# A one-core decoder layer: how its first transfers are queued and how its last norm is finished

## The chip, the cores and the metric

The kernel runs on one core of a Trainium2 chip. The metric is the device time of one launch in microseconds (us), taken as the median of several runs. A separate, profiled execution of the same program gives the trace that is read below.

## What is computed

One decoder layer on 512 tokens of width 1024, in float32. The input is multiplied by one wide matrix, whose columns are shared out among a gated spatial branch (A), a differential attention (B) and two merge gates. The result is projected, added to the scaled input and to a gated embedding, and normalized:

```
h = x @ w_in[i]
ua, va, za, qh, kh, vh, zb, ga, gb = jnp.split(h, IN_OFFSETS, axis=-1)
...
q = apply_rope(qh..., cos, sin) * (B_QK_DIM ** -0.5)      # cos, sin from positions
...
merged = jax.nn.sigmoid(ga) * (ya @ w_branch_a[i]) + jax.nn.sigmoid(gb) * (yb @ w_branch_b[i])
mix_out = merged @ w_out[i]
ple = jax.nn.sigmoid(x @ w_ple_gate[i]) * (p[i] @ w_ple[i])
x = layer_norm(DEEPNORM_ALPHA * x + mix_out + ple, ln_g[i], ln_b[i])
```

Two places matter here: the very first product (`x` times the columns of `k` and `q`), with the sine tables that are made from the positions beside it, and the `layer_norm` at the end.

## The kernel before

Every float32 operand of the large products is cut into a high and a low part (`cut`, lines 293 to 298: ScalarE copies the high part, VectorE subtracts to get the low one; for the first block of `x` VectorE does both). Each product is then three matmuls on TensorE. Weights come in units of 128 x 1024 floats from DRAM into `wr` buffers (line 360), and are cut into `wh` and `wl`.

**The start.** `x` arrives transposed, in eight blocks `xr[0]` to `xr[7]` of 128 x 512 (256 KB each, line 487), and the first product runs over these blocks in order: 12 matmuls for each block, which need that block and half of a weight unit. SyncE (the profile calls its queue SPq) issues the transfers in this order: `xr[0]`; `xr[1]`; the second half of unit 0; `xr[2]`; a half of unit 1; `xr[3]`; the other half of unit 1; `xr[4]`; and so on. ScalarE's queue issues the first half of unit 0, in two pieces, at the same time as SyncE issues `xr[0]`. `xr[1]` is held back by hand: GpSimd (POOL) writes one column of it with a memset (line 505), and the transfer that overwrites this column waits for that. Since SyncE issues in order, all its later transfers wait too. In GpSimd's queue the memset stands behind the making of `ident` and `mask` and two small constants. After the memset GpSimd issues five transfers of its own (lines 538 and 540): `invf` (128 frequencies) and `pos`, the 512 positions, each group of 128 of them repeated over 32 partitions. VectorE turns both into angles (lines 544 to 552) in the middle of its cuts, and from these come the tables of sines and cosines.

**In between.** The order of everything else is set by an agenda that counts matmuls: `later(n, fn)` runs `fn` after `n` more matmuls have been issued. It is not touched.

**The end.** The last product (`out`) gives four rows of 128 tokens, t = 0 to 3. For each, VectorE adds the product to `base` (line 1374), takes statistics (line 1375), and calls `last_norm`: aggregate them to mean and variance `mv` (line 1176); add epsilon to the variance, on GpSimd here (`ve`, line 1178); raise it to the power -0.5 on GpSimd (`rs`, line 1180); meanwhile VectorE subtracts the mean and multiplies by `lg` (line 1381), and then multiplies by `rs` and adds `lb` (line 1385); SyncE stores (line 1386). The last row's statistics come in three pieces (512, 256 and 256 columns), and it is stored in three: 512, 256 and 256 columns. The same `rstd_of` serves the norm in branch A, with VectorE adding the epsilon.

Of the kernel before, what the change touches and what calls it, by code (L numbers as in the profile page):

```python
# [18 lines left out]
OP = mybir.AluOpType  # L19
# [217 lines left out]
def hybrid_layer(ctx: ExitStack, tc: tile.TileContext, a, out: bass.AP):  # L237
# [248 lines left out]
    def ask_xr(k):  # L486
        sp.dma_start(out=xr[:, k, :], in_=a["xT"][k * P:(k + 1) * P, :])
# [2 lines left out]

    ident = consts.tile([P, P], F32, name="ident")
    make_identity(nc, ident)
    attn, turning = ExitStack(), ExitStack()
    ap_ = attn.enter_context(tc.tile_pool(name="attn", bufs=1))
    rp = turning.enter_context(tc.tile_pool(name="turning", bufs=1, side="right"))
# [5 lines left out]
    pool.memset(mhalf, -0.5)  # L501
    halfpi = consts.tile([P, 1], F32, name="halfpi")
    pool.memset(halfpi, math.pi / 2)

    pool.memset(xr[:, 1, 0:1], 0.0)
    for k in range(1, KT):
        ask_xr(k)
        if k < 6:
            next(arrive[k // 2])

    cs = rp.tile([P, T], F32, name="cs")
    sn = rp.tile([P, T], F32, name="sn")
# [14 lines left out]
    def rope_tables():  # L527

        pos = rp.tile([P, P], I32, name="pos", tag="m", bufs=6)
        ang = rp.tile([P, P], F32, name="ang", tag="m", bufs=6)  # L530
        n = rp.tile([P, P], F32, name="nn", tag="m", bufs=6)
        made = [rp.tile([P, P], F32, name="made", tag="m", bufs=6) for _ in range(2)]
        spread_out = dram.tile([2, P, P], F32, name="tables")
        magic = 1.5 * 2.0 ** 23
        near = float(np.float32(2 * math.pi))

        def ask_positions():
            pool.dma_start(out=invf, in_=a["invf"])
            for c in range(NT):
                pool.dma_start(out=pos[c * HALF:(c + 1) * HALF, :],  # L540
                             in_=bcast(a["pos"][:, c * P:(c + 1) * P], P, HALF))

        def angles():
            dve.tensor_copy(ang, pos)
            dve.tensor_scalar(out=ang, in0=ang, scalar1=invf[:, 0:1], scalar2=None, op0=OP.mult)

        def reduce(parts):
            dve.tensor_scalar(out=n, in0=ang, scalar1=1.0 / (2 * math.pi), scalar2=magic,
                              op0=OP.mult, op1=OP.add)
            dve.tensor_scalar(out=n, in0=n, scalar1=magic, scalar2=None, op0=OP.subtract)  # L550
            for c in parts:
                dve.scalar_tensor_tensor(out=ang, in0=n, scalar=-c, in1=ang, op0=OP.mult, op1=OP.add)

        def sines():
            pi32 = float(np.float32(math.pi))
            dve.tensor_scalar(out=ang, in0=ang, scalar1=pi32, scalar2=-pi32, op0=OP.min, op1=OP.max)
            dve.scalar_tensor_tensor(out=n, in0=ang, scalar=-1.0, in1=ang, op0=OP.mult, op1=OP.max)
            act.activation(made[0], ang, AF.Sin)
            act.activation(made[1], n, AF.Sin, bias=halfpi[:, 0:1], scale=-1.0)

        def put():
            for i, t in enumerate(made):
                act.dma_start(out=spread_out[i], in_=t)

        def get():
            for i, (queue, t) in enumerate(((sp, sn), (pool, cs))):
                for u in range(4):
                    queue.dma_start(out=t[u:P:4, :].rearrange("f (c j) -> f c j", c=NT),
                                   in_=spread_out[i].rearrange("(c f) j -> f c j", c=NT))

        ask_positions()
        yield
        angles()
        reduce(two_pi_parts())
        yield
        reduce((near, float(np.float32(2 * math.pi - near))))
        for after, fn in zip(TABLES, (sines, put, get)):
            later(after, fn)
        yield

    tables = rope_tables()
    next(tables)
    cuts = [prep(u, halves) for u in range(3)]
    cuts[0] = prep(0, (0, P, T, 2 * T))
    for k in range(KT):
# [585 lines left out]
    later(AUX[3], load_bs)  # L1171
    later(AUX[4], mask_ws)

    def rstd_of(st, eps_by=dve):
        mv = small([P, 2], "mv")
        dve.bn_aggr(out=mv, in_=st)  # L1176
        ve = small([P, 1], "ve")
        eps_by.tensor_scalar(out=ve, in0=mv[:, 1:2], scalar1=EPS, scalar2=None, op0=OP.add)  # L1178
        rs = small([P, 1], "rs")
        pool.tensor_tensor(out=rs, in0=ve, in1=mhalf[:, 0:1], op=OP.pow)  # L1180
        return mv, rs

    def va_done(c, t, z, source):
# [190 lines left out]
        dve.tensor_tensor(out=z, in0=bank, in1=z, op=OP.add)  # L1374
        dve.bn_stats(out=zst[t][:, piece if n == T else piece - 1, :], in_=z)

    def last_norm(t, cuts, stores):
        mv, rs = rstd_of(zst[t], pool)
        for c in cuts:
            z = base[:, t, c]  # L1380
            dve.scalar_tensor_tensor(out=z, in0=z, scalar=mv[:, 0:1], in1=lg[:, c],
                                     op0=OP.subtract, op1=OP.mult)
        for c in stores:
            z = base[:, t, c]
            dve.scalar_tensor_tensor(out=z, in0=z, scalar=rs[:, 0:1], in1=lb[:, c], op0=OP.mult, op1=OP.add)  # L1385
            sp.dma_start(out=out[t * P:(t + 1) * P, c], in_=z)
# [8 lines left out]
    for t in range(NT):  # L1395
        ts = slice(t * P, (t + 1) * P)
        n = T if t < NT - 1 else T // 2
        for j in range(T // n):
# [5 lines left out]
                m = slice((k % 2) * T + j * n, (k % 2) * T + (j + 1) * n)  # L1404
                three(bank[:, :n], mh[:, k, ts], ml[:, k, ts], h[:, m], l[:, m], k == 0, k == KT - 1)
            later(1, residual, t, T // n + j, n, bank[:, :n])
        whole, parts = [slice(0, D)], [slice(0, T), slice(T, T + 2 * P), slice(T + 2 * P, D)]
        later(1, last_norm, t, whole, whole if t < NT - 1 else parts)
    flush()


# [39 lines left out]
```

## Time and profile before

| | us |
|---|---|
| median of 3 runs (624.39 to 626.04) | 624.63 |
| the profiled execution's own time | 622.83 |
| its span, from the first to the last instruction | 621.1 |
| TensorE busy in the span | 610.3 (98%) |

The profiled execution took 622.83 us, of which 1.73 lie outside the span. It lies 1.80 below the median of the runs. Times in the rows below count from the start of the span. A matmul's recorded length overlaps the next one's, so back-to-back matmuls are read by their starts. "Idle before" is time in which an engine did nothing, with the instruction whose end released it.

### The profile page before, as it was taken

How to read it: one execution, taken by the hardware profiler on the slowest of the kernel's cores; microseconds unless marked ns; L12 is line 12 of the kernel's file. 1: busy time of each engine (PE TensorE's matmuls, PEld its weight loads, DVE VectorE, ACT ScalarE, POOL GpSimd, SP SyncE). 2: the span in 40 equal slices, each digit the busy share in tenths (PEclk: the TensorE clock that was granted, in tenths of full speed). 3: DMA queues.
4: the chain of work that ended last, by engine and by line, in shares of the span. 5: the costliest groups of instructions: out<-in, count | busy, mean ns of one | idle time of the engine just before them, and what ended most of it. 6: DMA issues, size and time to landing. Idle time of an engine off the chain costs nothing.

```text
span 621.1 us, 8650 instructions
## 1 busy us (share of the span) xinstructions
PE 610.3 (98%) x3036; PEld 514.0 (83%) x3036; DVE 456.1 (73%) x780; ACT 326.5 (53%) x528; POOL 137.5 (22%) x145
## 2 busy tenths in 40 slices
PE   8999999999999999999999999999999999999994
PEld 5888888888888888888889988888888888888884
DVE  5897876878878866856678978577667759476486
ACT  5546564554654655478666765557467446132200
POOL 2173114534534521321012120111210000000022
PEclk9999999999999999999999999999999999999998
DMA  8579999697796699669799898999988976752002
GB/s 280 205 198 209 282 307 293 228 250 242 232 242 231 197 325 267 171 233 302 276 286 260 224 244 229 242 249 306 254 197 278 363 247 230 257 182 102 1 34 102
DMA packets 49915, 143.77 MB, mean 231 GB/s; under 512 B 6416, under 2 KB 7760, under 8 KB 49552
## 3 DMA queue, kind: packets, MB, share of 16 engines
q1 hardware_dynamic: 38640, 109.99, 50.1%
q0 software_dynamic: 8352, 28.64, 25.2%
q10 hardware_dynamic: 2880, 4.59, 2.0%
q8 instruction: 24, 0.39, 0.3%
q14 instruction: 19, 0.16, 0.1%
HBM read 120.00 MB, written 34.73 MB: 249 GB/s over the span
## 4 chain that ended last, share of the span: by engine, by line
PE 96%; DVE 1%; DMA 1%; POOL 1%; ACT 0%; issue 0%; POOLq 0%; DVEq 0%; ACTq 0%
PE ps_pp L271 55%; PE ps_sc L271 18%; PE ps_tx L271 9%; PE ps_sc L820 3%; PE ps_po L865 3%; PE ps_po L271 3%; PE ps_tr L271 3%; PE ps_tr L854 1%; DMA xr<-in_xT 1%; PE ps_tr L1207 1%; PE ps_po L1207 1%; PE ps_tx L904 0%; POOL ve L1178 0%; DVE base L1385 0%; PE ps_pp L1354 0%; PE ps_sc L1354 0%
## 5 line engine op out<-in xcount | busy, mean ns | idle before, releaser
L403 DVE TENSOR_TENSOR wl<-wr,wh 128x1024 fp32r<-128x1024 f32 (+1 forms) x136 | 167.6, 1236 | 61.0 <-ACT wh L400 58.9
L400 ACT ACTIVATE wh<-wr 128x1024 fp32r<-128x1024 f32 (+1 forms) x136 | 139.6, 1033 | 79.2 <-PE ps_po L271 19.4
L271 PE MATMUL ps_pp<-xh,wh 128*128 128x512 f32 (+1 forms) x276 | 109.4, 398 | 1.5 <-ACT wh L297 1.5
L271 PE MATMUL ps_pp<-xl,wh 128*128 128x512 f32 (+1 forms) x276 | 106.7, 388 | 0.0
L271 PE MATMUL ps_pp<-xh,wl 128*128 128x512 f32 (+1 forms) x276 | 105.4, 383 | 0.0
L271 PEld LDWEIGHTS ps_pp<-xh,wh 128*128 128x128 f32 x276 | 52.3, 190 | 10.5 <-ACT wh L297 2.6
L833 ACT ACTIVATE p<-p,sth 128x128 f32<-128x128 f32 (+3 forms) x64 | 35.6, 557 | 46.5 <-DVE sth L831 46.5
L271 PEld LDWEIGHTS ps_pp<-xh,wl 128*128 128x128 f32 x276 | 52.1, 189 | 9.0 <-DVE wl L298 0.4
L271 PEld LDWEIGHTS ps_pp<-xl,wh 128*128 128x128 f32 x276 | 52.2, 189 | 7.4
L375 POOL DMA_DIRECT2D wr<-in_w x26 | 22.6, 870 | 106.1 <-DVE wl L403 81.3
L1178 POOL TENSOR_SCALAR ve<-mv 128x1 f32<-128x1 f32 x4 | 5.3, 1316 | 153.3 <-DVE mv L1176 153.3
L827 DVE CUSTOM_DVE_ANT_0 p<-ps_sc,mask 128x128 f32<-128x128 f32 (+3 forms) x64 | 31.0, 484 | 6.2 <-PE ps_sc L820 5.7
L271 PE MATMUL ps_pp<-wl,xh 128*128 128x512 f32 x84 | 32.9, 391 | 0.0
L271 PE MATMUL ps_pp<-wh,xl 128*128 128x512 f32 x84 | 32.8, 390 | 0.0
L271 PE MATMUL ps_pp<-wh,xh 128*128 128x512 f32 x84 | 32.7, 389 | 0.0
L271 PE MATMUL ps_sc<-wl,xsh 128*128 128x512 f32 x80 | 31.2, 390 | 0.0
L271 PE MATMUL ps_sc<-wh,xsl 128*128 128x512 f32 x80 | 31.1, 389 | 0.0
L271 PE MATMUL ps_sc<-wh,xsh 128*128 128x512 f32 x80 | 31.1, 389 | 0.0
L271 PE MATMUL ps_pp<-wh,xsh 128*128 128x512 f32 x64 | 24.9, 389 | 0.0
L271 PE MATMUL ps_pp<-wl,xsh 128*128 128x512 f32 x64 | 24.9, 389 | 0.0
L271 PE MATMUL ps_pp<-wh,xsl 128*128 128x512 f32 x64 | 24.9, 389 | 0.0
L865 PEld LDWEIGHTS ps_po<-v,at 128*128 128x128 f32 x160 | 22.8, 190 | 2.3
(367 smaller groups left out, 1418.6 us busy)
## 6 DMA issues: line engine op xcount, KB each, us to landing
wr<-in_w SPq DMA_DIRECT2D x83, 512.0 KB, 5.0
wr<-in_w POOLq DMA_DIRECT2D x22, 512.0 KB, 7.4
k<-hl SPq DMA_DIRECT2D x16, 256.0 KB, 2.6
q<-hl SPq DMA_DIRECT2D x16, 256.0 KB, 4.8
ws_va<-in_w POOLq DMA_DIRECT2D x8, 512.0 KB, 11.2
ws_wb<-in_w POOLq DMA_DIRECT2D x8, 512.0 KB, 8.3
wr<-ws_va SPq DMA_DIRECT2D x8, 512.0 KB, 8.2
wr<-ws_wb SPq DMA_DIRECT2D x8, 512.0 KB, 4.5
```

The lines of the kernel that those rows point to most:

```text
L271: pe.matmul(ps, s, m, start=start, stop=stop, skip_group_check=read_within)
L375: pool.dma_start(out=raw[u][:, :n], in_=weights(STEPS[FOLLOWS[u]][1], n), accum_op=OP.add)
L400: act.activation(h, raw[u][:, :width(STEPS[u][0])], AF.Copy)
L403: dve.tensor_tensor(out=l, in0=raw[u][:, :width(STEPS[u][0])], in1=h.bitcast(F32), op=OP.subtract)
L820: pe.matmul(sc[m][:, :n], q[:, m, i * P:(i + 1) * P], kk[:, m, :n], start=o == 0, stop=o == 1)
L827: dve.tensor_tensor_reduce(out=pr[m][:, :n], in0=sc[m][:, :n], in1=mask[:, T - n:], scale=-(DK ** -0.5), scalar=3e38, op0=OP.add, op1=OP.m ...
L833: act.activation(pr[m][:, :n], pr[m][:, :n], AF.Exp, bias=st[:, m:m + 1], scale=-1.0, accum_out=st[:, 2 + m:3 + m])
L854: pe.transpose(tr[:, j * P:(j + 1) * P], ad[:, j * P:(j + 1) * P], ident)
L865: pe.matmul(po[:, i * P:(i + 1) * P], at[:, j * P:(j + 1) * P], v[:, j, h * P:(h + 1) * P], start=j == 0, stop=j == i)
L1178: eps_by.tensor_scalar(out=ve, in0=mv[:, 1:2], scalar1=EPS, scalar2=None, op0=OP.add)
L1207: pe.matmul(sa[:, t * P:(t + 1) * P], va[:, t, g * P:(g + 1) * P], aux[0][:, 0, g, :], start=True, stop=True)
```

## The change

1. The memset that holds `xr[1]` back moves up in GpSimd's queue: it stands right behind the making of `ident`, ahead of `mask` and the constants.
2. The positions and frequencies are asked for by SyncE, in two transfers instead of five by GpSimd: `pos` in one, whose source lists 4 groups, each repeated 32 times, of 128 numbers; then `invf`. They stand behind the second half of unit 1, ahead of `xr[4]`.
3. VectorE adds the epsilon in the last norm too, into `mv` itself; the tile `ve` is gone (for branch A's norm as well, where VectorE did it already).
4. The last row is finished and stored in two pieces of 512 columns, and the subtraction of the mean (line 1381) is cut in two like that as well; before it was one instruction, followed by three pieces.

```
-    pool.memset(xr[:, 1, 0:1], 0.0)          (behind mask, mhalf, halfpi)
+    pool.memset(xr[:, 1, 0:1], 0.0)          (behind make_identity)
...
         def ask_positions():
-            pool.dma_start(out=invf, in_=a["invf"])
-            for c in range(NT):
-                pool.dma_start(out=pos[c * HALF:(c + 1) * HALF, :],
-                             in_=bcast(a["pos"][:, c * P:(c + 1) * P], P, HALF))
+            positions = a["pos"]
+            sp.dma_start(out=pos, in_=bass.AP(tensor=positions.tensor, offset=positions.offset,
+                                              ap=[[P, NT], [0, HALF], [1, P]]))
+            sp.dma_start(out=invf, in_=a["invf"])
...
     tables = rope_tables()
-    next(tables)
+    for k in range(1, KT):
+        ask_xr(k)
+        if k < 6:
+            next(arrive[k // 2])
+        if k == 3:
+            next(tables)
...
-    def rstd_of(st, eps_by=dve):
+    def rstd_of(st):
         mv = small([P, 2], "mv")
         dve.bn_aggr(out=mv, in_=st)
-        ve = small([P, 1], "ve")
-        eps_by.tensor_scalar(out=ve, in0=mv[:, 1:2], scalar1=EPS, scalar2=None, op0=OP.add)
+        dve.tensor_scalar(out=mv[:, 1:2], in0=mv[:, 1:2], scalar1=EPS, scalar2=None, op0=OP.add)
         rs = small([P, 1], "rs")
-        pool.tensor_tensor(out=rs, in0=ve, in1=mhalf[:, 0:1], op=OP.pow)
+        pool.tensor_tensor(out=rs, in0=mv[:, 1:2], in1=mhalf[:, 0:1], op=OP.pow)
...
-        whole, parts = [slice(0, D)], [slice(0, T), slice(T, T + 2 * P), slice(T + 2 * P, D)]
-        later(1, last_norm, t, whole, whole if t < NT - 1 else parts)
+        later(1, last_norm, t, [slice(0, D)] if t < NT - 1 else [slice(0, T), slice(T, D)])
```

SyncE's queue near its beginning, before, from `xr[2]` on (`wr_121` is unit 1, `wr_126` unit 2; a name in brackets is the semaphore that the transfer waits for: the transfers of SyncE and ScalarE take eight of them in turn, so each waits for the landing of the one eight places earlier):

```order
L487 DMA xr<-in_xT 128x512
L360 DMA wr_121<-in_w 128x512 [waits DMAHW0_49]
L487 DMA xr<-in_xT 128x512 [waits DMAHW1_49]
L360 DMA wr_126<-in_w 128x512 [waits DMAHW2_49]
L487 DMA xr<-in_xT 128x512 [waits DMAHW3_49]
L360 DMA wr_126<-in_w 128x512 [waits DMAHW4_49]
L487 DMA xr<-in_xT 128x512 [waits DMAHW5_49]
```

The same place in the changed kernel (`wr_127` is unit 1, `wr_140` unit 2):

```order
L487 DMA xr<-in_xT 128x512
L360 DMA wr_127<-in_w 128x512 [waits DMAHW0_49]
L535 DMA pos<-in_pos 128x1x128 [waits DMAHW1_49]
L537 DMA invf<-in_invf 128x1 [waits DMAHW2_49]
L487 DMA xr<-in_xT 128x512 [waits DMAHW3_49]
L360 DMA wr_140<-in_w 128x512 [waits DMAHW4_49]
L487 DMA xr<-in_xT 128x512 [waits DMAHW5_49]
```

The two small transfers have pushed `xr[4]` and all behind it by two places: `xr[4]` now waits for the semaphore of `xr[1]` (number 3), which `xr[5]` waited for before.

GpSimd's queue at its beginning, before:

```order
masks.py:199 AFFINE_SELECT ident<-ident 128x128 [waits Pool_49]
L497 MEMSET mask 128x512
L498 AFFINE_SELECT mask<-mask 128x128 [waits Pool_49]
L501 MEMSET mhalf 128x8
L503 MEMSET halfpi 128x1
L505 MEMSET xr 128x1
L538 DMA invf<-in_invf 128x1
L540 DMA pos<-in_pos 32x128 x4
```

And in the changed kernel:

```order
masks.py:199 AFFINE_SELECT ident<-ident 128x128 [waits Pool_49]
L494 MEMSET xr 128x1
L499 MEMSET mask 128x512
L500 AFFINE_SELECT mask<-mask 128x128 [waits Pool_49]
L503 MEMSET mhalf 128x8
L505 MEMSET halfpi 128x1
L564 DMA cs<-tables 32x4x128 [waits DMAHW0_49]
```

The memset of `xr` has moved ahead of four instructions, and the five transfers are gone.

VectorE's last instructions, before, from the last piece of the product on:

```order
L1374 TENSOR_TENSOR base<-ps_pp,base 128x256 [waits PE_49]
L1375 BN_STATS vst<-base 128x6 [waits DVE_49]
L1176 BN_AGGR mv<-vst 128x2 [waits DVE_49]
L1381 SCALAR_TENSOR_TENSOR base<-base,mv,lg 128x1024 [waits DVE_49]
L1385 SCALAR_TENSOR_TENSOR base<-base,rs,lb 128x512 [waits DVE_49,Pool_49]
```

And in the changed kernel:

```order
L1374 TENSOR_TENSOR base<-ps_pp,base 128x256 [waits PE_49]
L1375 BN_STATS vst<-base 128x6 [waits DVE_49]
L1177 BN_AGGR mv<-vst 128x2 [waits DVE_49]
L1178 TENSOR_SCALAR mv<-mv 128x1 [waits DVE_49]
L1381 SCALAR_TENSOR_TENSOR base<-base,mv,lg 128x512 x2
L1385 SCALAR_TENSOR_TENSOR base<-base,rs,lb 128x512 [waits DVE_49,Pool_49]
L1385 SCALAR_TENSOR_TENSOR base<-base,rs,lb 128x512 [waits DVE_49]
```

The epsilon has come in ahead of the subtraction of the mean, on the engine that does both; line 1385 still waits for GpSimd, where only the power is left.

## Rows read from the trace of the kernel before

**Rows 1.** Busy time of each engine in two stretches of the span: the stretch, its length, then for each engine the busy us and the number of instructions, the granted clock as a share of full speed, the DMA engines' share, and GB/s.

```profile
9.50:78.00 68.50, 68.50 (x301) 56.42 (x302) 58.56 (x81) 40.40 (x54) 22.23 (x20) 1.00 0.84 239
613.06:621.10 8.04, 0.00 (x0) 0.00 (x0) 3.95 (x8) 0.00 (x0) 1.88 (x2) 0.71 0.34 130
```

**Rows 2.** Everything that TensorE waited for in the whole span: us in total, times, longest.

```profile
PE ps_pp L271 <- ACT wh L297: 1.5, 1, 1.5
PE ps_po L475 <- DVE zeros L472: 1.2, 1, 1.2
```

**Rows 3.** The chain of work that ended last, at its beginning, in order of time: start, us, what.

```profile
1.36 0.49 POOL mask L497
...
2.30 0.04 POOL xr L505
...
2.36 5.72 DMA xr<-in_xT
...
8.17 0.63 ACT xh L297
...
8.82 0.64 ACT wh L297
...
9.50 2.61 PE ps_pp L271 x9
```

**Rows 4.** Transfers issued from 2.0 to 2.7 us (`xr[1]`), from 2.7 to 3.0 (the second half of unit 0), and in the first 10 us those of `pos`: size, and us from issue to landing (the median where there are several); below them GpSimd's timeline for the issue of `pos`: start, us.

```profile
xr<-in_xT SPq DMA_DIRECT2D x1, 256.0 KB, 5.7
...
wr<-in_w SPq DMA_DIRECT2D x1, 256.0 KB, 6.1
...
pos<-in_pos POOLq DMA_DIRECT2D x4, 16.0 KB, 6.5
...
3.04 2.29 POOL L540 DMA_DIRECT2D pos<-in_pos  x4
```

**Rows 5.** The last matmul of the first block of `x`, from TensorE's timeline: start, us.

```profile
7.59 0.39 PE L271 MATMUL ps_tx<-xh,wl 128*128 128x512 f32 x1
```

**Rows 6.** VectorE's cut of the weights for the block of `xr[4]`, and the first of its pairs of cuts for the third step of `v`; with, from the chain, TensorE's block of `xr[4]` and its first two steps of `v` on those banks (24 matmuls to a step); start, us.

```profile
13.94 0.69 DVE L298 TENSOR_TENSOR wl<-wr,wh 128x512 fp32r<-128x512 f32 x1
...
48.48 2.35 DVE L403 TENSOR_TENSOR wl<-wa,wh 128x1024 fp32r<-128x1024 f32 x2
...
18.24 2.04 PE ps_pp L271 x9
...
45.44 8.16 PE ps_pp L271 x36
```

**Rows 7.** The DMA engines in the first 10 us, in slices of 0.25 us: their busy share in tenths, and GB/s.

```profile
DMA  0000000934999965536938959579899999999999
GB/s 0 0 0 0 0 0 0 106 68 162 330 406 363 406 244 72 57 66 172 124 98 205 189 172 221 156 188 291 307 361 402 393 410 406 414 389 381 422 332 385
```

**Rows 8.** SyncE's queue: the issue of `xr[4]`, and that of `xr[5]`, eight transfers after `xr[1]`; start, us.

```profile
5.12 0.81 SPq L487 DMA_DIRECT2D xr<-in_xT  x1
...
8.10 0.33 SPq L487 DMA_DIRECT2D xr<-in_xT  x1
```

**Rows 9.** The chain of work that ended last, in its last part, in order of time: start, us, what.

```profile
614.02 0.25 DVE mv L1176
...
614.34 1.31 POOL ve L1178
...
616.34 0.75 DVE base L1385
```

**Rows 10.** The last row's instructions on VectorE (timeline), SyncE's last stores (timeline), and the transfers of line 1386 by size with us to landing.

```profile
614.29 1.29 DVE L1381 SCALAR_TENSOR_TENSOR base<-base,mv,lg 128x1024 f32<-128x1024 f32 x1
...
616.34 1.54 DVE L1385 SCALAR_TENSOR_TENSOR base<-base,rs,lb 128x512 f32<-128x512 f32 x3 [0.77 <-POOL rs L1180]
...
617.12 1.30 SPq L1386 DMA_DIRECT2D out<-base  x3
...
out<-base SPq DMA_DIRECT2D x3, 512.0 KB, 2.6
out<-base SPq DMA_DIRECT2D x1, 256.0 KB, 2.0
out<-base SPq DMA_DIRECT2D x2, 128.0 KB, 2.1
```

**Rows 11.** The norm of branch A, where VectorE adds the epsilon: VectorE's timeline around 356 us and GpSimd's power there; the same power at 320 us, where VectorE runs nothing of its kind; and, from the list of groups, the mean length of the cut of line 403 (us in total, mean ns).

```profile
355.84 0.15 DVE L1178 TENSOR_SCALAR ve<-mv 128x1 f32<-128x1 f32 x1
355.91 1.28 DVE L1194 SCALAR_TENSOR_TENSOR va<-va,mv,a_ln_g 128x1024 f32<-128x1024 f32 x1
357.10 1.22 DVE L403 TENSOR_TENSOR wl<-wr,wh 128x1024 fp32r<-128x1024 f32 x1
...
356.07 1.53 POOL L1180 TENSOR_TENSOR rs<-ve,mhalf 128x1 f32<-128x1 f32 x1 [4.16 <-DVE ve L1178]
...
320.48 0.57 POOL L1180 TENSOR_TENSOR rs<-ve,mhalf 128x1 f32<-128x1 f32 x1 [1.64 <-DVE ve L1178]
...
L403 DVE TENSOR_TENSOR wl<-wr,wh 128x1024 fp32r<-128x1024 f32 (+1 forms) x136 | 167.6, 1236 | 61.0 <-ACT wh L400 58.9
```

**Rows 12.** Small packets elsewhere: us to landing of the four transfers of `lamv` (32 KB each, one row of DRAM repeated over 128 partitions, issued by SyncE at 31 to 33 us; least, median, most); and ScalarE's queue from 24 to 27 us, when it only moves the tables in packets of 512 bytes: packets, MB, and the time that they took as a share of 16 engines over these 3 us.

```profile
DMA to landing us min/median/max: 6.0/8.9/10.3
...
q10 hardware_dynamic: 288, 0.13, 15.0%
```

More of the change, by code (lines that the diff above doesn't have):

```diff
@@ L492, in hybrid_layer @@
     make_identity(nc, ident)
+    pool.memset(xr[:, 1, 0:1], 0.0)
     attn, turning = ExitStack(), ExitStack()
@@ L503, in hybrid_layer @@
     pool.memset(halfpi, math.pi / 2)
[L505 to L509, printed above, removed]
     cs = rp.tile([P, T], F32, name="cs")
@@ L1375, in residual, with last_norm @@
         dve.bn_stats(out=zst[t][:, piece if n == T else piece - 1, :], in_=z)
-    def last_norm(t, cuts, stores):
-        mv, rs = rstd_of(zst[t], pool)
+    def last_norm(t, cuts):
+        mv, rs = rstd_of(zst[t])
         for c in cuts:
@@ L1382, in last_norm @@
                                      op0=OP.subtract, op1=OP.mult)
-        for c in stores:
+        for c in cuts:
             z = base[:, t, c]
```

## The prediction

> **What bounds the kernel now.** I read the busy time by stretches first, then what TensorE waits for, then the two ends of the chain that ended last, since only there is anything left. TensorE is busy in all of the 68.50 us after 9.50 us, and in nothing of the 8.04 us after 613.06 [rows 1]. In the whole span it waits twice: 1.2 us for its first operand and 1.5 us for ScalarE's `wh` [rows 2]. So from 9.50 to 613.06 the kernel is TensorE's own work. An edit pays only if it makes TensorE start its second block of `x` earlier without starving it later, or if it shortens the 8 us behind the last matmul.
>
> At the beginning the chain shows the hold itself: the mask's memset on GpSimd from 1.36, the memset of `xr` at 2.30, then the transfer of `xr[1]` from 2.36 for 5.72 us to 8.08, ScalarE's two copies (0.63 and 0.64), TensorE at 9.50 [rows 3]. The second copy reads the other half of unit 0, which landed 6.1 us after its issue at about 2.74, so at 8.8, just when ScalarE was ready for it [rows 4, 3]: both transfers are late together. TensorE's last matmul of the first block starts at 7.59 and another could follow 0.23 later (36 in a row take 8.16), at 7.82. So at most 9.50 - 7.82 = 1.68 us can be won there [rows 5, 6].
>
> **The change part by part: the start.** The memset now runs where the mask's stood, at 1.36 instead of 2.30: the transfers from `xr[1]` on are released 0.94 us earlier [rows 3]. What this gives TensorE has to be bounded. Upper end: 1.68, the room just worked out. Lower end: 0, if `xr[1]` lands when it landed before. Not below nothing: an earlier `xr[1]` shares the DMA engines with the first block's data, but its 256 KB at the 330 to 406 GB/s of that moment [rows 7] cost the first block 0.8 us at most, which would end it at 8.6, still ahead of 9.50. I take 0.9, the release itself carried through, because the row nearest to it is that of `xr[1]`, a fixed chain of issue, 5.7 us, two copies [rows 4, 3].
>
> The five transfers that GpSimd no longer issues were waited for by nobody on time: they landed some 6.5 us after their issue up to 5.3 us, before VectorE used them at 14.55, right behind the cut that starts at 13.94 [rows 4, 6]. On SyncE two come in, behind them `xr[4]` and all later loads. As the order shows, `xr[4]` now waits for the landing of `xr[1]`; in the trace `xr[5]` did that, issued at 8.10, just after 8.08 [rows 8, 3]. So `xr[4]` is issued at about 7.2 instead of 5.12 [rows 8]. But at 7.2 five transfers of 256 KB still stand ahead of it, 0.65 us each at 400 GB/s [rows 7], so with 0.3 us for the two small ones it lands near 11.4. I cost this at nothing, and the cover is VectorE's lead: it finished the weights of that block at 14.63 and TensorE begins it at 18.24, a lead of 3.6 us; the smallest lead that I find behind it is in the third step of `v`, which begins 5.44 after 45.44, at 50.88, with its first weights cut at 49.66 (half of the 2.35): 1.2 us [rows 6]. If VectorE's chain did not move forward at all, TensorE could still come 1.2 us earlier.
>
> **The end.** Taking GpSimd's 1.31 us for `ve` out of the chain [rows 9] looks like 1.2 us, and is less. That instruction ends at 615.65, 0.07 behind VectorE's line 1381, which ends at 615.58 [rows 9, 10]; VectorE itself does the same sum in 0.15 [rows 11]. So the 1.31 is a wait for VectorE's instruction. The power will wait the same way: in branch A's norm it started while VectorE ran an instruction of that form, took 1.53 instead of the 0.57 that it takes undisturbed, and ended at 357.60, 0.41 behind that instruction's end at 357.19 [rows 11]. Now step by step for the last row. `mv` ends at 614.27. The epsilon starts at 614.29, line 1381 0.07 behind it, as 355.91 follows 355.84: 614.36, so +0.07. Its two halves take 1.41: three pieces of line 1385 took 1.54, one whole instruction 1.29, so 0.13 for each further piece [rows 10]. They end at 615.77. The power gets in when the first half ends, at about 615.1, and ends 0.41 later, at 615.5, hidden. Line 1385 starts at 615.79 instead of 616.34, and its two pieces end at 617.20 instead of 617.88: 0.68 won. The last store is then 256 KB and not 128 KB; 256 KB landed in 2.0, 128 KB in 2.1 [rows 10], so I add 0.07: the end gives 0.75. Its bounds: upper 1.0, if the halves overlap so that two take 1.29 each and the store saves its 0.1. Lower -0.24: the power waits for both halves (615.77 + 0.41, line 1385 from 616.21 to 617.62, 0.26 won), and the last store, 0.7 behind another of its size, takes the 2.6 of 512 KB (0.5 lost).
>
> One rule speaks against this. After the power's turn at 357.19 VectorE's next cut, which reads two operands from SBUF, still takes 1.22, against a mean of 1.24: it was not held up [rows 11]. The Trainium skill (SBUF — State Buffer, section "SBUF: two separate sides") says that GpSimd and VectorE share a port pair as an exclusive lock, which the one that comes first keeps for its whole instruction. By that the second half of line 1381 would wait out the power, some 0.4 to 0.57 us, and the sum would be 0.5 smaller, near 623.5. The trace agrees on the waiting of GpSimd and not on that of VectorE behind a power; I go by the trace.
>
> **Sum.** 0.9 + 0.75 = 1.65 us. On the profiled execution, 622.83 becomes 621.18; its difference to the median (1.80) is carried over: 624.63 - 1.65 = 622.98, forecast 623.0.
>
> **Rivals.**
> A. It was GpSimd's own transfers that made `xr[1]` slow. For: after the first data (330 to 406 GB/s up to 3.5 us) the engines move only 57 to 221 from 3.75 to 6.75, which is when those five transfers were issued and taken up [rows 7, 4]; a transfer of that size takes 2.0 at the end [rows 10]. Against: the packets are few, and the slow stretch is as well explained by 16 engines starting anew. If so, `xr[1]` lands well before 6.4 and VectorE's chain moves forward with it, and the whole room of 1.68 is won: 624.63 - 1.68 - 0.75 = 622.2.
> B. The slow stretch keeps its place: whatever slows the engines until 6.75 is not moved by an earlier release. Then `xr[1]` lands at 7.9 or so. For: it lasts longer than the 256 KB need [rows 7]. Against: it follows the release in the trace, and earlier requests meet engines still at work. Start 0.2: 624.63 - 0.95 = 623.7.
> C. The slower side: the two small transfers in SyncE's row hold up `xr[4]`. Nearest row: four transfers of 32 KB with small packets took 6.0 to 10.3 us to land [rows 12], up to 8.3 more than the 2.0 of 256 KB. Then `xr[4]` lands at 11.4 + 8.3 = 19.7, and with two copies TensorE's block begins at 21.0 instead of 18.24: 2.8 lost, 0.75 won at the end, 626.7. It decides from where the block begins 0.75 late, so from `xr[4]` landing 6.3 us later than 11.4. Against: those four landed behind heavy traffic of GpSimd's queue.
> Packets of that kind cost 15.0% of 16 engines over 3 us for 288, 25 ns each [rows 12]. The Trainium skill (DMA: Bandwidth & Descriptors, section "Rules for kernel authors") says that a transfer whose outermost dimension has c < 16 steps uses at most c engines. `pos` lists 4 groups outermost, so an estimate by that page is 32 packets on each of four engines, 0.8 us instead of 0.2. That leaves C more than 5 us short of its point.
>
> **How the numbers follow.** The forecast 0.46, A 0.28, B 0.18, C 0.05, others 0.03. A measurement of this kernel can tell about 0.3%, 1.87 us, from no change. The forecast's 1.65 lies 0.2 below this line, with bounds on both sides: 0.3 of its chance lies over it. A's 2.43: 0.9. B's 0.95: 0.03. Faster: 0.14 + 0.25 + 0.01 = 0.40. C counts as slower for the most part: 0.04. Same: 0.56. Range: from A with some scatter, 621.8, to B with the end near its lower bounds, 624.4; C and the far ends stay outside.
>
> **What the profile after would show.** The memset of `xr` near 1.4 and the transfer behind it; `xr[1]` landing at 7.2 (forecast), below 6.4 (A) or near 8 (B); TensorE's second block at 8.6, 7.8 or 9.3. `xr[4]` issued right at the landing of `xr[1]`. TensorE without any new wait; one at the third step of `v` or at the block of `xr[4]` would prove the cover wrong. At the end, counted from the last `mv`: power over 0.41 behind the first half, line 1385 starting 1.5 after `mv`'s end. If the power ends behind the second half, or the second half is longer than 0.75, my reading of the shared wait is wrong. The forecast fails most easily in the 0.9, which the trace of before cannot split between the release and what follows it.

## The result, and the profile after

| | before | after |
|---|---|---|
| median, us (first timing, 11 runs each) | 624.86 | 621.18 (620.27 to 624.25) |
| ratio, with its 95% interval | | 0.9946 (0.9929 to 0.9964) |
| median, timed again in a later session (23 and 12 runs) | 624.04 | 622.17 (620.12 to 624.48) |
| ratio, with its 95% interval | | 0.9965 (0.9947 to 0.9983) |
| the profiled execution's own time | 622.83 | 620.35 |
| its span | 621.1 | 618.6 |

The change makes the kernel faster, by 3.7 us in the first timing and 1.9 in the second. Over all executions that were seen here (113 of before, 25 of after) the medians are 624.6 and 621.6: 3.0 us. The forecast was a gain of 1.65 and a time of 621.8 to 624.4; the first timing lies outside, the second inside.

Between the two first profiles 2.48 us were saved. TensorE's work ends 1.41 earlier (613.06 [rows 1] and 611.65), and what follows it takes 1.09 less (8.04 [rows 1] and 6.95). What TensorE waits for, after, in the whole span (us in total, times, longest), to be laid beside [rows 2]:

```profile
PE ps_po L475 <- DVE zeros L472: 1.3, 1, 1.3
PE ps_pp L271 <- ACT wh L297: 0.2, 1, 0.2
```

The wait of 1.5 has become 0.2, and it is at another place: inside the first block. The chain of waits at the start (start, us, what) no longer holds the memset or `xr[1]`, as it did in [rows 3]:

```profile
0.81 0.41 ACTq L360
1.22 0.03 issue
1.25 3.63 DMA wr<-in_w
4.88 0.02 issue
4.91 0.53 ACT wh L297
5.44 0.04 issue
5.48 0.99 PE ps_pp L271 x2
```

Now the second piece of unit 0 decides, which ScalarE issues: 192 KB that landed 3.6 us after the issue, and 3.1 before. The second block starts at 8.35 instead of 9.50, right behind the first. SyncE's timeline (start, us) beside [rows 8], and the DMA engines' first 10 us in slices of 0.25 us (busy share in tenths, GB/s) beside [rows 7]:

```profile
4.42 0.72 SPq L535 DMA_DIRECT2D pos<-in_pos  x1
5.18 0.43 SPq L537 DMA_DIRECT2D invf<-in_invf  x1
5.65 0.43 SPq L487 DMA_DIRECT2D xr<-in_xT  x1
```

```profile
DMA  0000000236998999998888999999999999999989
GB/s 0 0 0 0 0 0 0 98 119 164 338 350 269 363 283 332 334 350 270 320 320 328 360 377 303 361 393 352 352 418 385 377 382 375 375 318 281 303 270 352
```

`xr[4]`, which waits for the landing of `xr[1]`, is issued at 5.65. The stretch of 57 to 221 GB/s is gone: 270 to 393 in its place.

The end, from VectorE's timeline (start, us) and GpSimd's below it, beside [rows 9, 10]:

```profile
612.60 0.24 DVE L1177 BATCH_NORM_AGGREGATE mv<-vst 128x2 f32<-128x18 f32 x1
612.87 0.15 DVE L1178 TENSOR_SCALAR mv<-mv 128x1 f32<-128x1 f32 x1
612.94 1.41 DVE L1381 SCALAR_TENSOR_TENSOR base<-base,mv,lg 128x512 f32<-128x512 f32 x2
614.26 1.41 DVE L1385 SCALAR_TENSOR_TENSOR base<-base,rs,lb 128x512 f32<-128x512 f32 x2
```

```profile
613.16 0.92 POOL L1180 TENSOR_TENSOR rs<-mv,mhalf 128x1 f32<-128x1 f32 x1 [3.79 <-DVE mv L1178]
```

The power ends at 614.08, behind the first half of line 1381 and ahead of the second's end (614.35), and line 1385 waits for nothing more. From the end of `mv` (line 1177) to VectorE's end it takes 2.82 us; before it took 3.61.

### The profile page after: what moved, and what is told of

It is laid out like the page before. It is cut to its first block, busy times and chain, and to the rows that moved or that the text cites. A ratio compares the mean times of both kernels' runs of the same rounds, so it can differ in the third digit from the quotient of the medians.

```text
span 618.6 us, 8644 instructions
## 1 busy us (share of the span) xinstructions
PE 610.2 (99%) x3036; PEld 514.2 (83%) x3036; DVE 457.7 (74%) x784; ACT 326.1 (53%) x528; POOL 132.7 (21%) x136
## 4 chain that ended last, share of the span: by engine, by line
PE 98%; DMA 1%; DVE 0%; issue 0%; DVEq 0%; ACT 0%; ACTq 0%
PE ps_pp L271 56%; PE ps_sc L271 18%; PE ps_tx L271 9%; PE ps_sc L821 3%; PE ps_po L866 3%; PE ps_po L271 3%; PE ps_tr L271 3%; PE ps_tr L855 1%; DMA wr<-in_w 1%; PE ps_tr L1207 1%; PE ps_po L1207 1%; PE ps_tx L905 0%; PE ps_sc L1354 0%; PE ps_pp L1354 0%; DVE base L1385 0%
## 5 line engine op out<-in xcount | busy, mean ns | idle before, releaser
L1180 POOL TENSOR_TENSOR rs<-mv,mhalf 128x1 f32<-128x1 f32 x8 | 8.7, 1082 | 167.2 <-DVE mv L1178 163.0
```

The source lines that it names most:

```text
L1180: pool.tensor_tensor(out=rs, in0=mv[:, 1:2], in1=mhalf[:, 0:1], op=OP.pow)
```

## The experiments

Spans and starts below are from one profile each, medians from the timed runs, where there were any. "Third block" is the time at which TensorE begins the third block of `x`: it holds the waits of the first two blocks and what a slow clock cost in them. Behind it TensorE has the same work in all of them.

**The parts alone.** `e1` is the kernel before with only the memset moved, `e2` with only the positions moved to SyncE, `e3` with only the new end (the change's `rstd_of`, `last_norm` and its call). `e0` is the kernel before. The edits of `e1` and of `e2` to the kernel before (in `e2` the loop that issues `xr[1]` and the rest moves down with the positions; its order stays):

```diff
 make_identity(nc, ident)
+pool.memset(xr[:, 1, 0:1], 0.0)
...
-pool.memset(xr[:, 1, 0:1], 0.0)
 for k in range(1, KT):
```

```diff
-pool.dma_start(out=invf, in_=a["invf"])
-for c in range(NT):
-    pool.dma_start(out=pos[c * HALF:(c + 1) * HALF, :],
-                 in_=bcast(a["pos"][:, c * P:(c + 1) * P], P, HALF))
+positions = a["pos"]
+sp.dma_start(out=pos, in_=bass.AP(tensor=positions.tensor, offset=positions.offset,
+                                  ap=[[P, NT], [0, HALF], [1, P]]))
+sp.dma_start(out=invf, in_=a["invf"])
...
+    if k == 3:
+        next(tables)
```

> The kernel before with one edit: the memset that holds back xr[1] stands where the mask's memset stood (about 1.4 instead of 2.3 us). GpSimd still issues its five transfers, the end is the old one. Theory T1, GpSimd's five transfers made the first transfers slow: xr[1] still takes over 5 us, the stretch of 57 to 221 GB/s stays, second block of TensorE at 9.0 or later, at most 0.5 us won, time 0.999 to 1.000 of before. Theory T2, the earlier release itself: xr[1] lands near 5.5, the slow stretch is gone, second block near 8.4, 1.1 to 1.5 us won, time near 0.998 of before.

> The kernel before with one edit: positions in one transfer by SyncE (and invf), GpSimd issues nothing at the start; the memset of xr keeps its old place behind halfpi's, the end is the old one. T1: xr[1], released at 2.3, lands after about 4 us at 6.4, the slow stretch is gone, second block near 7.9, all of 1.5 to 2 us won, time 0.997 of before. T2: xr[1] lands at 8 as before, second block at 9.5, nothing won, time 1.000.

> The kernel before with the new end alone (epsilon by VectorE, last row in two pieces), old start. From the two profiles: 8.04 us behind the last matmul become 6.95, so 1.09 won, time 0.998 of before. If the gain of the changed kernel comes from the start alone, 1.000.

> The kernel before, unchanged, profiled once more. Its profiled execution took 622.83, its timed runs 624.0 to 626.4. If the start varies from run to run, this profile shows another start: second block later than 9.5, or TensorE's last matmul later than 613.06 by 1 to 3 us, with a wait of TensorE that the first profile did not have. If the difference is not in the kernel's own work, the span is again 621.1 within 0.3.

Measured on one chip, with before at 625.15 (29 runs, 622.29 to 629.02): `e1` 622.88, ratio 0.9977 (0.9955 to 0.9998), 621.22 to 627.29; `e2` 622.81, 0.9967 (0.9946 to 0.9987), 622.33 to 624.33; `e3` 624.17, 0.9977 (0.9956 to 0.9998). Each part brings something alone, and neither start theory is the whole. With the release alone `xr[1]` lands after 4.5 us, as T2 had it, but the second block starts at 9.01, since unit 0's second piece takes 4.6. With the positions alone `xr[1]` lands after 3.8 and the second block starts at 8.04, where T2 had no gain. The third block starts at 11.73 with the release alone, at 11.19 with the positions alone, and at 12.63 in the first profile of before.

The unexpected one is `e3`. Its start is that of before, and yet its third block came at 13.46. The unchanged kernel, profiled again as `e0`, had it at 13.93. So the first profile of before had a quick start.

**How much the start varies.** The unchanged kernels were profiled again (`e9`, `e11`: before; `e10`: after), and `e8` is the kernel before with work for TensorE in the wait:

```diff
     for bank, at in zip(first_kq, s):
         product(bank, part[:, at], m[:, 0, :], part is h and m is xh, False)
+for _ in range(8):
+    pe.matmul(idle, h[:, s[0]], xh[:, 0, :], start=True, stop=True)
```

> The kernel before with eight matmuls more, whose results nobody reads (unit 0's first weights on xh[0], into the bank of the opening zeros), between the first and the second block of x: TensorE has work, for 1.8 us, while it waits for xr[1]; nothing comes earlier. Theory T3, the wait itself costs more than its length: the second block restarts slowly (2.45 us instead of 2.04), and in some executions the granted clock then falls to one half for 3.4 us (1.6 us lost). Then this kernel has a second block of 2.04, no half clock at the start, no execution with a mean clock of 0.993, and a median 0.5 to 1.2 us below before, though its second block starts at 9.5 all the same. Rival: the half clock and the slow restart come from what stands before the wait, or from the data; then nothing changes, or the median rises by up to 0.1.

> The kernel before, unchanged, profiled a third time. If its start varies (second block at 9.50 and 9.52 in two profiles, 10.33 in the one with the new end; third block at 12.63, 13.93, 13.46), the third block starts at 12.6 to 14.5 here, on the average of the profiles 0.8 us or more above the first profile. If the first profile was typical: 12.6.

> The changed kernel, unchanged, profiled a second time. Third block at 11.07 in its first profile and at 10.61 in that of the kernel with three pieces, whose start is the same. T4, the new start varies little: third block at 10.5 to 11.2, no half clock; what stands above a span of 618.6 comes from a stall near 92 or near 337 us. Rival: third block above 11.5.

> The kernel before, unchanged, profiled a fourth time; expectations as for the third.

Before's third and fourth profiles have the third block at 14.94 and 13.33. In the third, TensorE waited 2.5 us and then lost its clock. Here are `e9`'s timeline of TensorE (start, us), and its stretches from that wait on (the stretch, its length, busy us of PE, PEld, DVE, ACT and POOL with counts, granted clock, DMA share, GB/s):

```profile
10.30 0.50 PE L271 MATMUL ps_pp<-xh,wh 128*128 128x512 f32 x1 [2.46 <-ACT wh L297]
...
12.05 0.63 PE L271 MATMUL ps_pp<-xl,wh 128*128 128x512 f32 x1
12.47 0.63 PE L271 MATMUL ps_pp<-xh,wl 128*128 128x512 f32 x1
12.90 0.63 PE L271 MATMUL ps_pp<-xh,wh 128*128 128x512 f32 x1
```

```profile
10.30:14.94 4.64, 4.64 (x13) 3.40 (x13) 4.39 (x7) 4.10 (x7) 0.00 (x0) 0.63 1.05 390
14.94:18.00 3.06, 3.06 (x15) 2.51 (x14) 2.79 (x11) 2.36 (x5) 0.00 (x0) 1.00 0.63 248
```

The matmuls start 0.43 apart instead of 0.23, at a mean granted clock of 0.63 (a part at 2.4 and a part at 1.2 GHz): 12 matmuls took 4.64 us, 3.13 in the first profile of before and 2.72 in the changed kernel. Before's second profile lost its clock in the same way. Of the 102 executions of before that were timed beside these kernels 20 had a mean granted clock of 0.994 or less, with a median of 626.4; the others had 624.0. Of 25 of the changed kernel none had. This mean does not tell where in the span the clock fell, and the slow first blocks of `e15` and `e17` (below) do not show in it.

`e8` shows it from the other side. None of its 12 runs had such a clock (at a share of one in five that would happen by chance in some 7% of cases); they spread from 624.33 to 626.73 (the 16 of before beside them from 622.72 to 628.89), and its second block took 2.72 up to the third. Yet its median is 625.48, ratio 1.0012 (0.9992 to 1.0032): in its profile the eight matmuls began at 8.58 and the second block behind them at 10.42, while ScalarE had that block's weights at 9.28. They cost 1.1 us there. So the run fits the theory for the slow restart and the clock, and not for the median.

**Which part of moving the positions.** Three variants of the changed kernel's start, and one of its end. `e4`, where GpSimd issues the two transfers; `e5`, where SyncE issues the old five; `e6`, with the memset behind the mask's; `e7`, with the old cuts of the last row. Their edits to the changed kernel, in this order:

```diff
-sp.dma_start(out=pos, in_=bass.AP(tensor=positions.tensor, offset=positions.offset,
+pool.dma_start(out=pos, in_=bass.AP(tensor=positions.tensor, offset=positions.offset,
...
-sp.dma_start(out=invf, in_=a["invf"])
+pool.dma_start(out=invf, in_=a["invf"])
```

```diff
+sp.dma_start(out=invf, in_=a["invf"])
+for c in range(NT):
+    sp.dma_start(out=pos[c * HALF:(c + 1) * HALF, :],
+                 in_=bcast(a["pos"][:, c * P:(c + 1) * P], P, HALF))
```

```diff
-pool.memset(xr[:, 1, 0:1], 0.0)
...
 pool.memset(mask, 0.0)
+pool.memset(xr[:, 1, 0:1], 0.0)
```

```diff
-later(1, last_norm, t, [slice(0, D)] if t < NT - 1 else [slice(0, T), slice(T, D)])
+whole, parts = [slice(0, D)], [slice(0, T), slice(T, T + 2 * P), slice(T + 2 * P, D)]
+later(1, last_norm, t, whole, whole if t < NT - 1 else parts)
```

> The changed kernel, but the one transfer of the positions and that of invf are issued by GpSimd instead of SyncE. T1a, what hurts at the start is that GpSimd's queue takes part at all: the second piece of unit 0 lands late (4 us and more after its issue), second block of TensorE at 8.8 to 9.6, time 1 to 2.5 us above the changed kernel and spread over 3 us or more from run to run. T1b, what hurts is five transfers with a fixed cost each: two of them cost less than half of it, under 0.8 us above the changed kernel, spread as there.

> The changed kernel, but SyncE issues the positions in four transfers and invf, as GpSimd did before: the same five, with the same small packets. T1a (GpSimd's queue): as the changed kernel within 0.5 us, with xr[4] and what stands behind it in SyncE's queue issued some 2 us later, covered. T1c, it is the small packets themselves, whoever issues them: first data slow again, 1 to 2.5 us above the changed kernel, and a wider spread.

> The changed kernel, but the memset that holds back xr[1] stands behind the mask's memset, near 1.9 us instead of 1.4. If xr[1] takes the DMA engines away from the first block's data (3.6 us for unit 0's second piece there, 3.1 with a release at 2.3): that piece lands in 3.1 to 3.4, the first block ends 0.2 to 0.5 earlier, second block at 7.8 to 8.2 instead of 8.35, time 0.2 to 0.5 us below the changed kernel. If the later xr[1] decides instead: second block at 8.4 or later, time the same or up to 0.5 us above.

> The changed kernel, but the last row is normed whole and stored in the old three pieces; VectorE adds the epsilon. By my reading of the shared wait the power now waits for the whole of line 1381, ends 0.41 behind it, and the first piece of line 1385 starts about 1.8 us behind the end of mv (1.41 in the changed kernel, 2.07 before); VectorE ends 3.3 us behind mv (2.82 and 3.61). If the halves are not what frees the power: 1.4 and 2.95.

With the medians 622.28 (`e4`, 8 runs), 622.98 (`e5`, 11) and 622.31 (`e6`, 6), and before at 624.29, the ratios are 0.9954 (0.9936 to 0.9972), 0.9972 (0.9957 to 0.9988) and 0.9961 (0.9944 to 0.9978). In `e4` the second piece of unit 0 was late beside GpSimd's transfers (size, us to landing):

```profile
xr<-in_xT SPq DMA_DIRECT2D x2, 256.0 KB, 3.9
wr<-in_w ACTq DMA_DIRECT2D x1, 192.0 KB, 4.7
wr<-in_w ACTq DMA_DIRECT2D x1, 64.0 KB, 3.2
```

4.7 instead of 3.6, and the second block at 9.17, as expected of a queue that disturbs by taking part. The time, 0.7 above the changed kernel's median over all its runs, fits the few transfers as well, and the later profiles of the changed kernel (4.5 and 4.6, below) show that 4.7 in one profile proves little. `e4` stays inconclusive. In `e5` the third block comes at 11.06, as in the changed kernel: issued by SyncE, the same small packets did this start no harm. But SyncE's queue is then late:

```profile
4.40 0.45 SPq L534 DMA_DIRECT2D invf<-in_invf  x1
5.13 2.95 SPq L536 DMA_DIRECT2D pos<-in_pos  x4
8.45 0.35 SPq L487 DMA_DIRECT2D xr<-in_xT  x1
```

`xr[4]` is issued at 8.45 instead of 5.65, and TensorE's waits (us in total, times, longest) show a new one:

```profile
PE ps_pp L271 <- ACT wh L400: 0.7, 1, 0.7
PE ps_pp L271 <- DVE wl L403: 0.5, 1, 0.5
PE ps_pp L271 <- ACT wh L297: 0.4, 1, 0.4
PE ps_tx L271 <- ACT s L651: 0.3, 1, 0.3
```

The first two are near 340, where other profiles have a like wait (last section); the row of `s`, at 58.12, stands in no profile of the changed kernel. At the third block `e5` stood level with the changed kernel's first profile, at 60 us it was 1.0 behind. So in this profile one transfer in place of four was not cosmetic. The only other wait for `s` is in `e7`, 0.2 us at 57.23: its third block came 0.46 earlier than the changed kernel's first, and by 60 us nothing of that was left. A start that is earlier still would meet this wait. `e6` has unit 0's second piece at 3.1 and the third block at 11.57: what the first block gains by a later release, the second loses.

`e7` prices the two edits of the end. Its timeline of VectorE, and GpSimd's power:

```profile
614.52 0.15 DVE L1178 TENSOR_SCALAR mv<-mv 128x1 f32<-128x1 f32 x1
614.59 1.28 DVE L1381 SCALAR_TENSOR_TENSOR base<-base,mv,lg 128x1024 f32<-128x1024 f32 x1
616.31 1.54 DVE L1385 SCALAR_TENSOR_TENSOR base<-base,rs,lb 128x512 f32<-128x512 f32 x3 [0.44 <-POOL rs L1180]
...
614.82 1.45 POOL L1180 TENSOR_TENSOR rs<-mv,mhalf 128x1 f32<-128x1 f32 x1 [3.79 <-DVE mv L1178]
```

With the row normed whole, line 1385 starts 1.8 behind the end of `mv` (line 1177), as expected (2.07 before, 1.41 after): the power ends 0.40 behind the whole of line 1381. Of the 0.66 by which line 1385 starts earlier in the changed kernel, the epsilon's move is worth 0.26 and the halves 0.40.

**Release and positions together.** Each alone seemed to remove the long wait, so they were profiled again and then compared directly:

```diff
 make_identity(nc, ident)
-pool.memset(xr[:, 1, 0:1], 0.0)
```

This is `e12`, the changed kernel with no hold at all; `e16` has the line again, at its old place behind that of `halfpi`. `e13` is `e1`, `e14` is `e2`, `e15` and `e17` are the changed kernel.

> The changed kernel without the memset that holds back xr[1]: SyncE issues xr[0], xr[1] and the rest as fast as it can. If xr[1] takes the DMA engines from the first block's data (unit 0's second piece landed after 3.1 us with the release at 2.3 and 1.9, 3.3 to 3.6 at 1.4): it lands after 4 us or more, the first block ends later, third block at 11.3 to 12 instead of 10.6 to 11.2, median 0.3 to 1 us above the changed kernel. If only the start of xr[1] counts: third block at 10.6 or before, same median.

> The earlier release alone, unchanged, profiled a second time (third block at 11.73 in the first). If GpSimd's transfers still make the start vary: unit 0's second piece again lands after 4.5 us or more, third block between 11.7 and 13.5. If the release alone is enough: third block at 11.0 to 11.7, no half clock.

> The positions by SyncE alone, unchanged, profiled a second time (third block at 11.18 in the first). If GpSimd's transfers were the cause: third block at 11.0 to 11.6 again, no half clock. If the late release still lets the start vary: above 12.

> The changed kernel, unchanged, profiled a third time. Third block at 10.6 to 11.3, no half clock; rival: above 11.6.

> The changed kernel with the memset that holds back xr[1] at its old place (2.3 us): positions by SyncE and the new end stay. If the earlier release only adds spread: unit 0's second piece lands after 3.1 to 3.2, third block at 11.1 to 11.6, no execution with half clock in the first block, median as the changed kernel or up to 0.5 us below, least time some 0.3 us above it. If the earlier release is worth what its first profile showed: median 0.3 to 0.8 us above the changed kernel.

> The changed kernel, unchanged, on the same chip as the kernel with the late release, for the comparison. Third block between 10.6 and 13.3; spans from 618.6 to 622.5 as in its first runs, wider than those of the late release.

All starts but that of `e8`, the profiles of one kind in one row (`e7` has the start of the changed kernel, `e16` that of `e2`; in `e5` SyncE issues the five):

| kind (profiles) | release, us | GpSimd's transfers | unit 0's second piece, us to landing | `xr[1]`, us to landing | third block, us | mean |
|---|---|---|---|---|---|---|
| before, `e0`, `e9`, `e11`, `e3` | 2.3 | 5 | 3.1, 3.1, 3.2, 3.1, 3.2 | 5.7, 5.8, 6.5, 6.4, 6.5 | 12.63, 13.93, 14.94, 13.33, 13.46 | 13.66 |
| `e1`, `e13` | 1.4 | 5 | 4.6, 3.9 | 4.5, 4.1 | 11.73, 11.26 | 11.50 |
| `e2`, `e14`, `e16` | 2.3 | 0 | 3.1, 3.1, 3.1 | 3.8, 4.1, 4.6 | 11.19, 11.34, 11.62 | 11.38 |
| after, `e10`, `e15`, `e17`, `e7` | 1.4 | 0 | 3.6, 3.6, 4.5, 4.6, 3.3 | 4.0, 4.0, 4.5, 4.6, 3.7 | 11.07, 11.24, 13.27, 13.50, 10.61 | 11.94 |
| `e5` | 1.4 | 0 | 3.9 | 4.0 | 11.06 | |
| `e6` | 1.9 | 0 | 3.1 | 4.6 | 11.57 | |
| `e4` | 1.4 | 2 | 4.7 | 4.7 | 11.89 | |
| `e12` | none | 0 | 4.1 | | 13.08 | |

Two things stand out. `xr[1]` took 5.7 us or more only where it was released late and GpSimd issued its five transfers beside it. Here it is in `e9` and, released as late but without those transfers, in `e14`:

```profile
xr<-in_xT SPq DMA_DIRECT2D x1, 256.0 KB, 6.5
...
xr<-in_xT SPq DMA_DIRECT2D x1, 256.0 KB, 4.1
```

And unit 0's second piece took 3.1 or 3.2 wherever the release stood at 1.9 or later, and 3.3 to 4.7 in all ten profiles with an earlier one or none.

The rival to T4 (that the new start varies little) came true in `e15` and `e17`: the changed kernel can start as late as before. `e17`'s chain:

```profile
1.25 4.62 DMA wr<-in_w
...
5.89 0.53 ACT wh L297
6.42 0.04 issue
6.47 1.22 PE ps_pp L271 x2
7.69 0.43 PE ps_tx L271
8.12 1.28 PE ps_pp L271 x3
```

Unit 0's second piece took 4.62, TensorE ran dry for 1.2 us behind its first real matmul, and most of the first block then ran at 0.43 a matmul, the spacing of the half clock above (here the view of stretches lists a clock of 1.00). That the dry spell brings the slow matmuls is not shown: `e4` ran dry for 1.3 us and `e1` for 1.1 without them, `e12` for 0.4 with them. With the old release TensorE did not run dry there in three profiles; `e16`'s timeline of TensorE:

```profile
5.73 0.40 PE L271 MATMUL ps_tx<-xh,wh 128*128 128x512 f32 x1
5.96 0.85 PE L271 MATMUL ps_pp<-xl,wh 128*128 128x512 f32 x3
...
8.47 0.50 PE L271 MATMUL ps_pp<-xh,wh 128*128 128x512 f32 x1 [0.52 <-ACT wh L297]
```

`e16` has 621.64 (620.75 to 623.72), ratio 0.9960 (0.9943 to 0.9977); the changed kernel beside it 622.17 (620.12 to 624.48), 0.9965 (0.9947 to 0.9983). The two can't be told apart in the median; in these twelve runs each the late release has the narrower spread. No hold at all gives 622.89, 0.9979 (0.9961 to 0.9997), and the slow first block again. No version was found that beats the changed kernel by more than can be measured.

## Why the prediction was wrong

**The direction was right. The start's size and cause were wrong, the end was sized too low, and a distance was carried over that belonged to one execution.** By the prediction's own steps:

- *The start's 0.9, "the release itself carried through"*: the step that failed. It took the 5.7 us of `xr[1]` for fixed and had it land at 7.2. In the changed kernel `xr[1]` took 4.0 and had landed by 5.65; TensorE no longer waited for it, and the end of the first block decided. Between the two first profiles the start gave 1.41. The second block starts 1.15 earlier: the room of 1.68, less 0.53 by which the first block ends later. Then it takes 2.72 up to the third and not 3.13: restarting behind a wait cost 0.41, which I left out though it stood in the rows (from start to start the nine matmuls of [rows 3] took 2.45, where the chain lists 2.61, and later ones 2.04 in [rows 6]). Some 0.15 is lost again, for the most part from 471 to 481 us. Over the profiles of each kind the third block came 1.7 earlier (13.66 and 11.94).
- *Whose gain it is.* I put it on the release, and gave the transfers of GpSimd (rival A) 0.28. With the old release and no transfer of GpSimd the third block comes at 11.38 on the mean; with the release alone at 11.50; with both at 11.94. The two edits are substitutes: the long wait for `xr[1]` needed a late release and GpSimd's transfers at once, and with either edit alone the second block waits some 0.5 us or less (`e1` waits 1.1 inside the first block instead). The medians agree: the release alone won 2.3, the positions alone 2.3 and the end alone 1.0, 5.6 in sum, and all together 3.0. Rival A had the mechanism of the slow `xr[1]` and nearly the price (the second block at 8.04, 8.21 and 8.47 without GpSimd's transfers; 7.8 was forecast for A), but not that the earlier release alone escapes those transfers. The second edit added nothing that these runs can show.
- *"Not below nothing"*: wrong for single executions. I let the earlier `xr[1]` cost the first block 0.8 at most and end it by 8.6. It did cost it: 0.5 in the first profile, and in `e15` and `e17` the first block ended at 10.5 and 10.8, where TensorE ran dry and then worked slowly. I had priced the bytes and not the slow matmuls.
- *The difference of profile and median, 1.80, "carried over"*: wrong. The first median of after lies 0.83 above its profile, not 1.80; this 0.97 is more than half of the 1.80 by which the first timing lies below the forecast, and more than the errors of the start (0.51) and of the end (0.34) between the first profiles together. The profile of before had the earliest third block of five; only 8 of its 113 timed executions were as quick as its 622.83. The clock is a part of before's excess: one execution in five had the low mean, and these were 2.4 us slower. That the second timing's 1.9 lies near the forecast does not bear it out: the profile beside it, `e17`, has the slow first block, which the forecast did not have.
- *`xr[4]` at nothing*: right. It was issued at 5.65, not the 7.2 that I worked out, and no wait of TensorE came of it in the first profile. `e5` shows where that cover ends: issued at 8.45, with all later loads behind it, TensorE had lost 1.0 us by 60 us in its one profile. Rival C's place was right; its price was not tested.
- *The end's 0.75*: mis-sized, 1.09 in the profiles. Line 1385 started 1.41 behind `mv` and not 1.52, since its first half overlaps the end of line 1381 (0.11), and the last of two stores is issued sooner behind VectorE's end than the last of three (its issue ends at 616.02, 0.35 behind; before at 618.42, 0.54 behind). The rest, 0.1, is the store's landing.
- *The shared wait, and the rule against it*: right. The power ended some 0.4 behind the first half (0.41 forecast), and the halves took 1.41 together, not 0.4 to 0.57 more. `e7`, where there is no first half, put the power behind the whole instruction.
- *Rival B* (the slow stretch keeps its place): wrong. In the changed kernel it is gone, and `xr[1]` had landed by 5.65. With the release alone (`e1`) the slices that had 57 to 221 GB/s show 181 to 391.

What stays open: by what means GpSimd's transfers slow those that other queues issue beside them (`xr[1]`, released at 2.3, took 5.7 to 6.5 with them and 3.8 to 4.6 without), why the changed kernel's 192 KB take 3.6 in one execution and 4.6 in another (the profiles come from several chips, and no run separates the chip from chance), and what decides whether a wait of 1.5 to 2.5 us costs the clock: it did in two of five profiles.

## What to carry to other kernels

One profile of a program's first ten microseconds is one draw: profile an unchanged kernel two or three times before pricing a gain there, and don't carry one execution's distance from the median over to the changed kernel. A wait of TensorE costs its length, a slow restart that the next rows show, and in some executions a stretch at half clock: `e0`'s wait of 1.84 us cost 3.5, since the block behind it took 4.41 and not 2.72. Before adding up two edits on one wait, ask whether each alone would remove it; the second then brings nothing, and here it may have brought spread. The duration of a transfer in one trace is no constant: ask what was issued beside it.

## What the runs showed of the hardware

Two other places make executions of either kernel differ by 1 to 3 us. One is at 92 us. In `e10`, VectorE's timeline and GpSimd's:

```profile
91.67 6.75 DVE L403 TENSOR_TENSOR wl<-wr,wh 128x1024 fp32r<-128x1024 f32 x1
```

```profile
91.49 0.81 POOL L332 DMA_DIRECT2D ws_va<-in_w  x1 [2.75 <-DMA ws_va<-in_w]
92.04 1.58 POOL L755 TENSOR_TENSOR m<-m 128x512 f32<-128x512 f32 x1
93.29 1.57 POOL L756 TENSOR_TENSOR m<-m 128x512 f32<-128x512 f32 x1
94.53 2.80 POOL L766 TENSOR_TENSOR hl<-m,hl 128x512 fp32r<-128x512 f32 x2
```

A cut that takes 1.24 on the mean [rows 11] took 6.75: it started 0.18 behind an issue of GpSimd and ended 1.09 behind the last of GpSimd's four operations that followed without a gap; TensorE waited 1.2 us at 102. In the changed kernel's first profile the same cut started 0.69 ahead of that issue and took 1.22, and GpSimd's four operations came behind it. That the long cut waited for GpSimd is read from these times; no run tests it. The Trainium skill (SBUF — State Buffer, section "SBUF: two separate sides") has one engine wait for the other's whole instruction; here the cut ended only behind four, which the page does not say. `e4` and `e7` had the same, and in `e8` it met the instruction ahead of the cut. The other place is 337 to 340: an accumulating transfer that GpSimd issues near 329 landed after 8.1 to 9.0 us, and TensorE waited 1.0 to 1.9 us (`e6`, `e13`; `e5` and `e14` have the same wait); in the changed kernel's first profile it took less than 6. In `e13` the matmuls behind the wait then ran at a mean granted clock of 0.55, from 340.3 to 344.0. Neither was met in the first two profiles.
